# HGRN heads in seven pieces: transposes behind the level runs, the samples' work joined to the halves' turn-backs

## The chip, the cores and the metric

The kernel runs on one core of a Trainium2 chip. The metric is the device time of one execution in microseconds (us); less is better. The engines are named as the profile names them: PE (matrix products; PEld is its weight load), DVE (elementwise work), ACT (activations and copies), POOL (elementwise work), SP (issues most transfers). A change within about 0.2% (2.3 us) can't be told from no change here.

## The reference

One layer of a hybrid model on 1024 prompt tokens and 8 samples of 8 tokens: `h = x + W_out(concat[mLSTM(n), HGRN2(n)])` with `n = RMSNorm(x)`, then a last RMSNorm. Four mLSTM heads and eight HGRN2 heads, all in float32. Each HGRN2 head of 128 channels computes, in chunks:

```python
def step(S, inp):
    qc, kc, vc, fc = inp
    b = jnp.cumsum(fc, 2)
    diff = b[:, :, :, None, :] - b[:, :, None, :, :]
    D = jnp.exp(jnp.where(causal, diff, -jnp.inf))
    A = jnp.einsum('bhtk,bhsk,bhtsk->bhts', qc, kc, D)
    o = jnp.einsum('bhts,bhsv->bhtv', A, vc) + jnp.einsum('bhtk,bhkv->bhtv', qc * jnp.exp(b), S)
    kd = kc * jnp.exp(b[:, :, -1:] - b)
    S_new = jnp.exp(b[:, :, -1])[..., None] * S + jnp.einsum('bhsk,bhsv->bhkv', kd, vc)
    return S_new, o
```

Its output is normalised per head and multiplied into a gate `z`; the result goes through `W_out`. The outputs also hold the new states of prompt and samples.

## The kernel before

**Products.** A float32 product is made of three passes over split operands (`mm3`, L94 to L96: high by high, high by low, low by high), each at most 512 columns wide. The input projection takes most of PE's time.

**Two streams on PE.** For every head there is a *main* generator (`hgrn_main`, `mlstm_main`) that makes the head's own work in pieces and yields a weight after each, and a *side* generator that makes the projection of heads to come in steps of six products, and in the last head the beginning of the output stage. `weave` runs a piece of main, then as many side steps as its weight is worth. The heads run H0 M0 H1 M1 H2 M2 H3 M3 H4 H5 H6 H7 (H for HGRN2, M for mLSTM). The constant HEAD says what all weights of a head add up to. PE runs in the order in which the code is written. DVE, ACT, POOL and SP run in an order that a scheduler lays out by its own costs, each engine strictly in its order.

**An HGRN head's pieces.** First a burst of 32-wide products for level 1 of a tree of scores, then a run for levels 2 to 16 (`level_run(lower)`), each after DVE has made the levels' factors (`products`, L1030 to L1035). The nine transposes of the values (L1105) give `Vt`; ACT copies them (L1107) and makes the samples' masked copies VH, VL. `level_run(upper)` makes levels 32 and 64; ACT copies their scores into `A` (L1079). The keys, decayed on DVE into `KD` (L1110 to L1112), are turned by nine transposes (L1136) and copied by ACT into `KDt` (L1138) and, for the samples, into `KS` (L1142, subtracted on DVE at L1144). Then the prompt's state products (L1182) and the chain of eight states on DVE (L1190, L1192), whose last state SP stores (L1194). Then `outputs(0)` and `outputs(1)`, the two halves of the prompt (L1201, L1204), each normalised by `normed`: square on ACT (L1150), sum on DVE (L1152), root on POOL (L199, L200), multiply on DVE (L1154). The multiplied tile is turned back on PE (L1163, `turned`) and multiplied into `z` on DVE (L1211, `onto_z`). The samples' outputs are L1220 and L1225, their states L1232, L1233 (PE) and L1236 (DVE).

**Buffers.** PSUM pools: `lv` with two buffers (bursts, first transposes, turn-backs), `o` with three (states, outputs, values' transposes), `mm` with three (projection). A new tile waits for the last reader of the tile that held its buffer.

**What follows an HGRN head.** An mLSTM head begins with three loads on SP (RB L684, q L685, k L686); DVE adds into DT from RB (L691, L693); ACT takes Exp of DT and of RB (L694, L695), with a table load before the first and another before the sigmoid of `om` (L648) behind them. Later `pair_prep` loads `vr` (L704).

Of the kernel before, what the change touches and what calls it, by code (L numbers as in the profile page):

```python
# [13 lines left out]
ALU = mybir.AluOpType  # L14

P = 128
DM = 1024
T = 1088
# [12 lines left out]
def hybrid_step(  # L31
# [909 lines left out]
    def hgrn_main(h):  # L941
# [43 lines left out]
        def small_out(ps, o, li, n):  # L985
            W = MASKW[li]
            if li == 0:
                V.copy_predicated(A32, MK[0], ps[:, o:o + W])
            else:
                dst = A32[:, :2 * W].rearrange("p (g two n) -> p g two n", two=2, n=n)[:, :, 1, :]  # L990
                V.copy_predicated(dst, MK[li].rearrange("p (g n) -> p g n", n=n),
                                  ps[:, o:o + W].rearrange("p (g n) -> p g n", n=n))
# [12 lines left out]
        def rhs2(r, j):  # L1005
            if r == 4:
# [9 lines left out]
        ps = ps_lv()  # L1016
        burst(small_mms(ps, 0, K1[:, 0:512], k[:, TP:T], rhs1, 32)
              + small_mms(ps, 288, K1[:, 512:1024], k[:, TP:T], rhs2, 16), (q1, k1, k2))
        small_out(ps, 0, 0, 1)
        small_out(ps, 288, 1, 1)  # L1020
        late = [deferred.pop(0) for _ in range(len(deferred))]
# [14 lines left out]
                            hv(f, W, n)[:, :, 0, n - 1:n].to_broadcast([P, ng, n]), op=ALU.mult)  # L1036
            return n, Qn, Kn, last

        def level_run(group):
            ps = ps_lv()  # L1040
            mms, outs, o = [], [], 0
            for n, Qn, Kn, last in group:
                if n <= 16:
                    def rhs(r, j, Qn=Qn):
                        if r == 4:
                            return Qn[:, 512 + 16 * j:512 + 16 * j + 16]
                        return pairs(Qn, r * P + 16 * j, 112 - 32 * j, 2, 1, 16)

                    mms += small_mms(ps, o, Kn, Kn[:, 512:576] if n <= 4 else None, rhs, 16)
                    outs.append((n, o))  # L1050
                    o += MASKW[LEVELS.index(n) + 1]
                else:

                    for r in range(4):
                        for j in range(4):
                            b = 32 * j // n
                            odd, g = b % 2, (P // n - 1 - b if b % 2 else b) // 2
                            c = r * P + 64 * odd + n * g
                            mms.append((ps[32 * j:32 * j + 32, o + r * n:o + (r + 1) * n],
                                        Kn[:, r * P + 32 * j:r * P + 32 * j + 32], Qn[:, c:c + n], True, True))  # L1060
                    outs.append((n, o))
                    o += 4 * n
            burst(mms, (last,))
            for n, o in outs:
                if n <= 16:
                    small_out(ps, o, LEVELS.index(n) + 1, n)
                    if n == 16:

                        for j in range(4):
                            a = A[32 * j:32 * j + 32, 32 * j:32 * j + 1]  # L1070
                            dst = bass.AP(a.tensor, a.offset, [a.ap[0], [256, 4], [224 - 64 * j, 2], [1, 32]])
                            S.copy(dst, A32[32 * j:32 * j + 32, 0:256].rearrange("p (r e c) -> p r e c", e=2, c=32))  # L1072
                        for g in range(2):
                            S.copy(A[64 * g:64 * g + 32, TP + 32 * g:TP + 32 * g + 32], A32[64 * g:64 * g + 32, 256:288])
                else:
                    for b in range(P // n):
                        odd, g = b % 2, (P // n - 1 - b if b % 2 else b) // 2
                        c = P * odd + n * (2 * g + 1)
                        S.copy(A[n * b:n * b + n, 0:TP].rearrange("p (r c) -> p r c", r=4)[:, :, c:c + n],  # L1079
                               ps[n * b:n * b + n, o:o + 4 * n].rearrange("p (r c) -> p r c", r=4))  # L1080
# [8 lines left out]
            yield 3.3  # L1089
        upper = [products(16)]  # L1090
        yield 2.0
        level_run(lower)
        if h == 4:
            norm_states()
        yield 2.0
        for n in (32, 64):
            upper.append(products(n))
            yield 3.0
        V.tensor_tensor(q[:, :T], q[:, :T], f[:, :T], op=ALU.mult)
        Vt = unit("V")  # L1100
        for kk in range(3):
            pt = ps_o()
            for u in range(4 if kk < 2 else 1):
                t = kk * 4 + u
                PE.transpose(pt[:, u * P:(u + 1) * P], iT[:, t * P:(t + 1) * P], ident)  # L1105
            w = 512 if kk < 2 else P
            S.copy(Vt[:, kk * 512:kk * 512 + w], pt[:, :w])  # L1107
        KD = iT
        kdp = KD[:, :TP].rearrange("p (r two c) -> p r two c", two=2, c=P)
        V.tensor_tensor(kdp[:, :, 0, :], kp[:, :, 0, :], sfp[:, :, 0, :], op=ALU.mult)  # L1110
        V.tensor_tensor(kdp[:, :, 1, :][:, :, ::-1], kp[:, :, 1, :], sfp[:, :, 1, :], op=ALU.mult)
        V.tensor_tensor(twice(KD[:, TP:U]), once(k[:, TP:T]), once(Sf[:, TP:T]), op=ALU.mult)  # L1112

        Vs, VH, VL = half("Vs", F32R), half("VH", F32R), half("VL", F32R)
        S.copy(Vs[:, :P], Vt[:, TP:U])
# [8 lines left out]
        S0 = unit("S0")  # L1124
        S0v = S0[:, :1024].rearrange("p (b c) -> p b c", c=P)
        nc.sync.dma_start(out=S0v, in_=st_S[0, :, h].rearrange("b k v -> k b v"))
        yield 3.3
        level_run(upper)
        yield 3.4
        KDt = unit("KDt")  # L1130
        KS = two_groups()
        for kk in range(3):
            pt = ps_lv() if kk < 2 else ps_o()
            for u in range(4 if kk < 2 else 1):
                t = kk * 4 + u
                PE.transpose(pt[:, u * P:(u + 1) * P], KD[:, t * P:(t + 1) * P], ident)  # L1136
            if kk < 2:
                S.copy(KDt[:, kk * 512:(kk + 1) * 512], pt)  # L1138
            else:
                for g in range(2):  # L1140
                    r, c = slice(64 * g, 64 * g + 64), slice(g * P, (g + 1) * P)
                    S.copy(KS[r, c], pt[r, :P])  # L1142
                    r = slice(64 * g + 32, 64 * g + 64)
                    V.tensor_tensor(KS[r, c], pt[r, :P], f32(KS[r, c]), op=ALU.subtract)  # L1144
        yield 2.0

        def normed(ps, w):

# [9 lines left out]

        def turned(sq, w):

            tp = ps_lv()
            for u in range(w):
                PE.transpose(tp[:, u * P:(u + 1) * P], sq[:, u * P:(u + 1) * P], ident)  # L1163
            return tp
# [27 lines left out]
                V.scalar_tensor_tensor(Sn, states[-1], f[:, j * P + 127:j * P + 128], pk, op0=ALU.mult, op1=ALU.add)  # L1192
            states.append(Sn)
        nc.sync.dma_start(out=o_pS[0, 0, h], in_=states[7])  # L1194
        yield 3.2

        def outputs(hb):
            pq = ps_o()
# [13 lines left out]
            last_split(hb * 512, 512)  # L1212

        sq0 = outputs(0)
        yield 2.6
        sq1 = outputs(1)
        yield 2.6
        pq = ps_o()
        for j in range(4):
            PE.matmul(pq[32 * j:32 * j + 32, :P], lhsT=A[:, TP + win(j):TP + win(j) + 32],  # L1220
# [1 line left out]
        for e in range(2):  # L1222
            for j in range(4):
                b = 2 * j + e
                PE.matmul(pq[32 * j:32 * j + 32, :P], lhsT=qm[:, b * 64 + win(j):b * 64 + win(j) + 32], rhs=S0v[:, b, :],  # L1225
                          start=False, stop=e == 1)
        sq8 = normed(pq, 1)
        onto_z(sq0, 0)
        yield 2.6
        for g in range(2):  # L1230
            pk = ps_o()
            PE.matmul(pk, lhsT=KS[:, g * P:(g + 1) * P], rhs=VH[:, :512], start=True, stop=False)  # L1232
# [4 lines left out]
                                       pk[:, a * P:(a + 1) * P], op0=ALU.mult, op1=ALU.add)  # L1237
        nc.sync.dma_start(out=o_sS[0, :, h].rearrange("b k v -> k b v"), in_=S0v)
        onto_z(sq1, 1)
        yield 2.4  # L1240
        tp = turned(sq8, 1)
        zz, ts = compact(z[:, TP:T]), spread(tp[:, :P])
        for a in range(2):
# [133 lines left out]
            yield from g  # L1377

    STEPS = 48
    HEAD = {"H": 48.6, "M": 48.2}  # L1380

    def weave(side, main, ratio):

# [162 lines left out]
```

## Time and profile before

| what | value |
|---|---|
| median of 3 runs | 1164.46 us (1164.11 to 1165.91) |
| profiled execution | 1163.69 us |
| its span | 1161.9 us |
| mean granted PE clock | .993 |
| PE busy, 0 to 240 us | 216.06 |
| PE busy, 240 to 404 us | 162.57 of 164.00 |
| PE busy, 404 to 900 us | 491.96 of 496.00 |
| PE busy, 900 to 1162 us | 252.29 of 262.00 |
| DVE, ACT, POOL busy | 744.4, 467.4, 259.5 |

The profiled execution's time is its span and 1.8 us around it. PE is nearly full while the heads run (240 to 900 us), and has some 10 us idle in the last part, where the output stage waits for loads and splits. In the quoted rows, a start time in us is followed by the duration, engine, line, operation, `out<-in` with the program's names, and, in brackets, the idle time before it with what ended it. A row "x4" is four instructions in one, and starts with the first.

### The profile page before, as it was taken

How to read it: one execution, taken by the hardware profiler on the slowest of the kernel's cores; microseconds unless marked ns; L12 is line 12 of the kernel's file. 1: busy time of each engine (PE TensorE's matmuls, PEld its weight loads, DVE VectorE, ACT ScalarE, POOL GpSimd, SP SyncE). 2: the span in 40 equal slices, each digit the busy share in tenths (PEclk: the TensorE clock that was granted, in tenths of full speed). 3: DMA queues.
4: the chain of work that ended last, by engine and by line, in shares of the span. 5: the costliest groups of instructions: out<-in, count | busy, mean ns of one | idle time of the engine just before them, and what ended most of it. 6: DMA issues, size and time to landing. Idle time of an engine off the chain costs nothing.

```text
span 1161.9 us, 22940 instructions
## 1 busy us (share of the span) xinstructions
PE 1122.9 (97%) x9251; PEld 1055.8 (91%) x9251; DVE 744.4 (64%) x1474; ACT 467.4 (40%) x1045; POOL 259.5 (22%) x403
## 2 busy tenths in 40 slices
PE   5889999999999999999999999999999999999997
PEld 5789999899999999999999999999999997878886
DVE  4665354394778567784779467878677686644443
ACT  5454454426432443244422453252424344343332
POOL 4352443101530044203520153111020200100000
PEclk9889999999999999999999999999999999999999
DMA  7234343213324242324124331322222255475662
GB/s 238 70 120 142 118 147 122 76 45 115 102 81 151 63 147 78 117 94 135 56 78 151 118 108 60 133 74 77 56 77 56 76 162 151 143 231 163 200 188 95
DMA packets 154296, 134.05 MB, mean 115 GB/s; under 512 B 11515, under 2 KB 130391, under 8 KB 154190
## 3 DMA queue, kind: packets, MB, share of 16 engines
q1 hardware_dynamic: 154190, 132.59, 36.6%
q8 instruction: 73, 1.20, 0.4%
q14 instruction: 33, 0.27, 0.1%
HBM read 93.99 MB, written 38.57 MB: 114 GB/s over the span
## 4 chain that ended last, share of the span: by engine, by line
PE 78%; DVE 8%; ACT 5%; DMA 5%; issue 2%; SPq 0%; POOL 0%; POOLq 0%; DVEq 0%; ACTq 0%
PE mm L94 22%; PE mm L95 21%; PE mm L96 21%; PE lv L101 2%; DMA woraw<-in_w_out 1%; DMA mraw<-mixd 1%; ACT A L1079 1%; DMA RB<-rd 1%; ACT A L1072 1%; PE o L1182 1%; PE o L94 1%; PE o L96 1%; PE o L95 1%; PE o L1201 1%; PE o L1204 1%
## 5 line engine op out<-in xcount | busy, mean ns | idle before, releaser
L94 PE MATMUL mm<-XH,whi 128*128 128x384 f32 (+1 forms) x1344 | 451.7, 336 | 2.2 <-DVE xml L470 2.0
L95 PE MATMUL mm<-XL,whi 128*128 128x384 f32 (+1 forms) x1344 | 440.2, 328 | 0.0
L96 PE MATMUL mm<-XH,wlo 128*128 128x384 f32 (+1 forms) x1344 | 439.7, 327 | 0.0
L94 PEld LDWEIGHTS mm<-XH,whi 128*128 128x128 f32 x1344 | 253.8, 189 | 5.7 <-DVE xml L470 2.2
L95 PEld LDWEIGHTS mm<-XL,whi 128*128 128x128 f32 x1344 | 253.9, 189 | 1.6 <-issue 1.3
L96 PEld LDWEIGHTS mm<-XH,wlo 128*128 128x128 f32 x1344 | 253.3, 188 | 0.0
L147 POOL TENSOR_TENSOR wlo<-wraw,whi 128x1024 fp32r<-128x1024 f32 x34 | 83.0, 2442 | 108.6 <-ACT whi L147 108.4
L147 ACT CAST whi<-wraw 128x1024 fp32r<-128x1024 f32 x56 | 58.9, 1051 | 105.2 <-PE mm L95 84.7
L948 POOL MEMSET A<- 128x288 f32 x8 | 2.7, 342 | 251.0 <-ACT A L1072 251.0
L96 PE MATMUL mm<-XH,mlo 128*128 128x512 f32 x144 | 56.5, 392 | 1.1 <-DVE mlo L1295 1.0
L94 PE MATMUL mm<-XH,mhi 128*128 128x512 f32 x144 | 57.2, 397 | 0.2 <-ACT mhi L1294 0.2
L1294 ACT CAST mhi<-mraw 128x1024 fp32r<-128x1024 f32 (+1 forms) x32 | 31.8, 997 | 61.1 <-PE mm L95 38.6
L95 PE MATMUL mm<-XL,mhi 128*128 128x512 f32 x144 | 56.1, 390 | 0.0
L1295 DVE TENSOR_TENSOR mlo<-mraw,mhi 128x1024 fp32r<-128x1024 f32 (+1 forms) x32 | 36.9, 1155 | 24.7 <-ACT mhi L1294 24.5
L896 DVE TENSOR_SCALAR f<-f,OML,LB 128x384 f32<-128x384 f32 (+1 forms) x24 | 33.6, 1401 | 28.7 <-ACT f L894 28.6
L470 DVE TENSOR_TENSOR xml<-mm,xmh 128x384 fp32r<-128x384 f32 (+1 forms) x24 | 12.3, 511 | 51.0 <-ACT XB L469 48.0
L1363 POOL TENSOR_TENSOR rs<-rs,mhalf 128x1 f32<-128x1 f32 (+1 forms) x9 | 4.9, 542 | 147.7 <-DVE rs L1362 147.7
L96 PE MATMUL mm<-woh,mlo 128*128 128x512 f32 x96 | 37.5, 390 | 0.4 <-DVE mlo L1295 0.4
L95 PE MATMUL mm<-wol,mhi 128*128 128x512 f32 x96 | 37.4, 389 | 0.0
L94 PE MATMUL mm<-woh,mhi 128*128 128x512 f32 x96 | 37.3, 389 | 0.0
L199 POOL TENSOR_SCALAR oss<-oss 128x4 f32<-128x4 f32 (+1 forms) x24 | 4.6, 192 | 145.7 <-DVE oss L1152 145.7
L486 DVE SCALAR_TENSOR_TENSOR Y<-XB,PAR,Y 128x1112 f32<-128x1112 f32 x24 | 36.8, 1533 | 0.3
(349 smaller groups left out, 2217.1 us busy)
## 6 DMA issues: line engine op xcount, KB each, us to landing
wraw<-in_w_in SPq DMA_DIRECT2D x56, 512.0 KB
woraw<-in_w_out SPq DMA_DIRECT2D x16, 512.0 KB
mraw<-mixd SPq DMA_DIRECT2D x16, 512.0 KB
mraw<-mixd SPq DMA_DIRECT2D x16, 448.0 KB
xcd<-XB SPq DMA_DIRECT2D x8, 544.0 KB
qkd<-qk SPq DMA_DIRECT2D x16, 272.0 KB
xcr<-xcd SPq DMA_DIRECT2D x8, 544.0 KB
mixd<-xcr SPq DMA_DIRECT2D x8, 544.0 KB
```

The source lines that it names most:

```text
L94: PE.matmul(out, lhsT=lh, rhs=rh, start=first, stop=False)
L95: PE.matmul(out, lhsT=lh, rhs=rl, start=False, stop=False)
L96: PE.matmul(out, lhsT=ll, rhs=rh, start=False, stop=last)
L101: i = PE.matmul(out, lhsT=lhsT, rhs=rhs, start=start, stop=stop)
L147: return S.copy(hi, raw), eng.tensor_tensor(lo, raw, f32(hi), op=ALU.subtract)
L470: evs.append(V.tensor_tensor(ml[:, t0:t0 + m], ps[:, :m], f32(mh[:, t0:t0 + m]), op=ALU.subtract))
L486: V.scalar_tensor_tensor(Y[:, :1112], XB[:, j:j + 1112], cw[:, 8 * j + ft:8 * j + ft + 1], Y[:, :1112], op0=ALU.mult, op1=ALU.add)
L896: V.tensor_scalar(f[:, s], f[:, s], scalar1=OML[:, h:h + 1], scalar2=LB[:, h:h + 1], op0=ALU.mult, op1=ALU.add)
L1072: S.copy(dst, A32[32 * j:32 * j + 32, 0:256].rearrange("p (r e c) -> p r e c", e=2, c=32))
L1079: S.copy(A[n * b:n * b + n, 0:TP].rearrange("p (r c) -> p r c", r=4)[:, :, c:c + n], ps[n * b:n * b + n, o:o + 4 * n].rearrange("p (r c) - ...
L1294: S.copy(hi[:, :w * n], raw[:, :w * n])
L1295: V.tensor_tensor(lo[:, :w * n], raw[:, :w * n], f32(hi[:, :w * n]), op=ALU.subtract)
```

## The change

The pieces of an HGRN head go from eleven to seven:

1. the level-1 burst (for head 4 with `norm_states`, which was behind the lower run);
2. `level_run(lower)`, with the nine transposes of the values straight behind its burst;
3. `level_run(upper)`, with the nine transposes of the keys straight behind its burst; of their three PSUM tiles the first is in `lv` and two in `o` (before, two in `lv` and one in `o`);
4. the prompt's states;
5. `outputs(0)`;
6. `outputs(1)`, the samples' outputs, and the first half's turn-back;
7. the samples' states, the second half's turn-back, and that of the samples, whose tile is now in `o`.

The weights of the pieces change with it (their sum, HEAD, from 48.6 to 46.7), and the product of q and f on DVE goes behind the keys' products. No product is added or taken away.

```diff
@@ level_run @@
-        def level_run(group):
+        def level_run(group, then=None):
...
             burst(mms, (last,))
+            if then:
+                then()
@@ behind products(16) @@
-        level_run(lower)
-        if h == 4:
-            norm_states()
-        yield 2.0
+        Vt = unit("V")
+
+        def turn_values():
+            for kk in range(3):
+                pt = ps_o()
+                for u in range(4 if kk < 2 else 1):
+                    t = kk * 4 + u
+                    PE.transpose(pt[:, u * P:(u + 1) * P], iT[:, t * P:(t + 1) * P], ident)
+                w = 512 if kk < 2 else P
+                S.copy(Vt[:, kk * 512:kk * 512 + w], pt[:, :w])
+
+        level_run(lower, turn_values)
+        yield 2.6
         for n in (32, 64):
             upper.append(products(n))
             yield 3.0
-        V.tensor_tensor(q[:, :T], q[:, :T], f[:, :T], op=ALU.mult)
...
         V.tensor_tensor(twice(KD[:, TP:U]), once(k[:, TP:T]), once(Sf[:, TP:T]), op=ALU.mult)
+        V.tensor_tensor(q[:, :T], q[:, :T], f[:, :T], op=ALU.mult)
...
-        yield 3.3
-        level_run(upper)
-        yield 3.4
+        yield 3.8
...
-            pt = ps_lv() if kk < 2 else ps_o()
...
+        def turn_keys():
+            for kk in range(3):
+                pt = ps_o() if kk else ps_lv()
...
+        level_run(upper, turn_keys)
+        yield 3.2
...
-            tp = ps_lv()
+            tp = ps_lv() if w > 1 else ps_o()
...
         nc.sync.dma_start(out=o_pS[0, 0, h], in_=states[7])
-        yield 3.2
+        yield 4.2
...
         sq0 = outputs(0)
-        yield 2.6
+        yield 4.2
         sq1 = outputs(1)
-        yield 2.6
...
+        onto_z(sq0, 0)
         sq8 = normed(pq, 1)
-        onto_z(sq0, 0)
-        yield 2.6
+        yield 4.2
...
         onto_z(sq1, 1)
-        yield 2.4
         tp = turned(sq8, 1)
...
-    HEAD = {"H": 48.6, "M": 48.2}
+    HEAD = {"H": 46.7, "M": 48.2}
```

Line numbers shift: of those that the prediction names, L1079 is L1084 after, L1136 L1142, L1138 L1144, L1150 to L1154 are L1158 to L1162, L1163 is L1171, L1201 L1209, L1211 L1219, L1220 L1227, L1232 L1239; up to L960 nothing shifts.

The engines that a scheduler lays out are ordered anew. On ACT, where head 1 ends and the first exponentials of the second mLSTM head are taken (`osq` are the squares of the first half, the second half and the samples; DT and RB are the mLSTM head's; `om` is a sigmoid of the projection), before:

```order
L1150 ACTIVATE osq_4543<-o_4535 128x512
L648 ACTIVATE om_4509<-mm_4516 128x384
L1150 ACTIVATE osq_4573<-o_4564 128x512
L694 ACT_TABLE_LOAD
L694 ACTIVATE DT_4685<-DT_4685 128x1088
L695 ACTIVATE RB_4679<-RB_4679 128x1088
L1150 ACTIVATE osq_4605<-o_4592 128x128
L648 ACT_TABLE_LOAD
L648 ACTIVATE om_4509<-mm_4557 128x384
```

and after:

```order
L648 ACTIVATE om_4509<-mm_4516 128x384
L1158 ACTIVATE osq_4550<-o_4542 128x512
L694 ACT_TABLE_LOAD
L694 ACTIVATE DT_4685<-DT_4685 128x1088
L695 ACTIVATE RB_4679<-RB_4679 128x1088
L648 ACT_TABLE_LOAD
L648 ACTIVATE om_4509<-mm_4557 128x384
L1158 ACTIVATE osq_4592<-o_4583 128x512
L1158 ACTIVATE osq_4618<-o_4599 128x128
```

The second half's square stood ahead of the first table load, and now stands behind the two exponentials, the second table load and a sigmoid.

On DVE at the same place (`oss` are the sums of the squares), before:

```order
L1152 TENSOR_REDUCE oss_4545<-osq_4543 128x4
L1154 TENSOR_TENSOR osq_4543<-o_4535,oss_4545 128x512
L691 SCALAR_TENSOR_TENSOR DT_4685<-RB_4679,COLS,CF 128x128 x8
L693 SCALAR_TENSOR_TENSOR DT_4685<-RB_4679,COLS,CF 128x64
L1152 TENSOR_REDUCE oss_4575<-osq_4573 128x4
L1211 SCALAR_TENSOR_TENSOR z_3559<-lv_4612,PAR,z_3559 128x512
L800 TENSOR_REDUCE w_736_5288<-DT_4685 128x1
L1154 TENSOR_TENSOR osq_4573<-o_4564,oss_4575 128x512
```

and after:

```order
L1150 TENSOR_TENSOR KS_4387<-o_4451,KS_4387 32x128
L1200 SCALAR_TENSOR_TENSOR St_4499<-St_4499,f_3555,o_4489 128x128
L1200 SCALAR_TENSOR_TENSOR St_4499<-St_4499,f_3555,o_4494 128x128 x4
L1160 TENSOR_REDUCE oss_4552<-osq_4550 128x4
L691 SCALAR_TENSOR_TENSOR DT_4685<-RB_4679,COLS,CF 128x128 x8
L693 SCALAR_TENSOR_TENSOR DT_4685<-RB_4679,COLS,CF 128x64
L1162 TENSOR_TENSOR osq_4550<-o_4542,oss_4552 128x512
L800 TENSOR_REDUCE w_736_5288<-DT_4685 128x1
L1160 TENSOR_REDUCE oss_4594<-osq_4592 128x4
L1160 TENSOR_REDUCE oss_4620<-osq_4618 128x1
L1219 SCALAR_TENSOR_TENSOR z_3559<-lv_4612,PAR,z_3559 128x512
L1162 TENSOR_TENSOR osq_4592<-o_4583,oss_4594 128x512
```

The first half's multiply (L1154, now L1162) stood ahead of the nine DT sums, and now stands behind them; a subtraction for KS now stands inside the chain of the states.

On SP, where head 0 ends and the first mLSTM head's loads are issued, before:

```order
L140 DMA wraw_3359<-in_w_in 128x8x128
L1194 DMA out<-St_2958 128x128
L684 DMA RB_3139<-rd 128x1088
L685 DMA q_3137<-qkd 128x1088
L686 DMA k_3138<-qkd 128x1088
L614 DMA out<-co_3009 3x1024
L615 DMA out<-co_3009 24x1024
L704 DMA vr_3192<-vd 128x516
```

and after:

```order
L140 DMA wraw_3359<-in_w_in 128x8x128
L1202 DMA out<-St_2931 128x128
L704 DMA vr_3192<-vd 128x516
L684 DMA RB_3139<-rd 128x1088
L685 DMA q_3137<-qkd 128x1088
L686 DMA k_3138<-qkd 128x1088
L614 DMA out<-co_3089 3x1024
L615 DMA out<-co_3089 24x1024
```

The load of `vr` has moved from behind the three loads and two stores to ahead of them.

More of the change, by code (lines that the diff above doesn't have):

```diff
@@ L1018, in hgrn_main @@
               + small_mms(ps, 288, K1[:, 512:1024], k[:, TP:T], rhs2, 16), (q1, k1, k2))
+        if h == 4:
+            norm_states()
         small_out(ps, 0, 0, 1)
@@ L1098, in hgrn_main @@
             yield 3.0
-        V.tensor_tensor(q[:, :T], q[:, :T], f[:, :T], op=ALU.mult)
[L1100 to L1107, printed above, removed]
         KD = iT
@@ L1126, in hgrn_main @@
         nc.sync.dma_start(out=S0v, in_=st_S[0, :, h].rearrange("b k v -> k b v"))
-        yield 3.3
-        level_run(upper)
-        yield 3.4
+        yield 3.8
         KDt = unit("KDt")
         KS = two_groups()
-        for kk in range(3):
-            pt = ps_lv() if kk < 2 else ps_o()
[L1134 to L1145, printed above, removed]
+        def turn_keys():
+            for kk in range(3):
+                pt = ps_o() if kk else ps_lv()
+                for u in range(4 if kk < 2 else 1):
+                    t = kk * 4 + u
+                    PE.transpose(pt[:, u * P:(u + 1) * P], KD[:, t * P:(t + 1) * P], ident)
+                if kk < 2:
+                    S.copy(KDt[:, kk * 512:(kk + 1) * 512], pt)
+                else:
+                    for g in range(2):
+                        r, c = slice(64 * g, 64 * g + 64), slice(g * P, (g + 1) * P)
+                        S.copy(KS[r, c], pt[r, :P])
+                        r = slice(64 * g + 32, 64 * g + 64)
+                        V.tensor_tensor(KS[r, c], pt[r, :P], f32(KS[r, c]), op=ALU.subtract)
+        level_run(upper, turn_keys)
+        yield 3.2
         def normed(ps, w):
```

## The prediction

> **What bounds the kernel now.** I read the busy shares first, then the chain that ended last, then TensorE's waits.
>
> ```profile
> PE 1122.9 (97%) x9251; PEld 1055.8 (91%) x9251; DVE 744.4 (64%) x1474; ACT 467.4 (40%) x1045; POOL 259.5 (22%) x403
> PE 78%; DVE 8%; ACT 5%; DMA 5%; issue 2%; SPq 0%; POOL 0%; POOLq 0%; DVEq 0%; ACTq 0%
> PE lv L1136 <- ACT A L1079: 4.7, 8, 1.1
> PE o L1232 <- DVE osq L1154: 1.8, 3, 1.1
> PE mm L96 <- DVE mlo L1295: 1.4, 3, 0.7
> ```
>
> TensorE (PE) is busy 97% and holds 78% of the chain. The last three rows (line waited for, us in total, times, longest) are the waits in the code that the change touches. So the time is PE's instruction stream plus its waits, and a change that leaves every product in place can move only two things: the waits, and the seams where PE passes from one kind of product to another. I price both against the profiled execution, 1163.69 us, which is 0.77 us under the median of 1164.46.
>
> **Gain 1: the keys' transposes.** Around them, in head 1 (start, us, engine, line):
>
> ```profile
> 395.91 0.60 PE L1136 MATMUL lv<-CF,iT 128*128 128x128 f32 x4
> 397.00 0.66 PE L1136 MATMUL lv<-CF,iT 128*128 128x128 f32 x4 [0.48 <-ACT A L1079]
> 397.52 0.39 PE L94 MATMUL mm<-XH,whi 128*128 128x320 f32 x1
> 397.75 0.31 PE L95 MATMUL mm<-XL,whi 128*128 128x320 f32 x1
> 397.89 0.31 PE L96 MATMUL mm<-XH,wlo 128*128 128x320 f32 x1
> ```
>
> The second group of four waits for ACT to copy the upper levels' scores out (L1079), since that frees the second `lv` buffer. The change puts this group into the `o` pool, where nothing has been held since the values' transposes. From 397.00 to 397.52 five transposes take .52, so four take .42, and the start distance of 1.09 holds .67 of wait: .48 in the row and .19 inside the modelled end. Over 8 heads that is the 4.7 of the waits plus 8 x .19: **-6.2** (bounds -4.7 and -6.2).
>
> **Gain 2: seams.** Leaving the transposes, L94 to L95 takes .23 where .14 is the pace of the next pair. Entering a burst of 32-wide products costs the same:
>
> ```profile
> 391.59 0.34 PE L96 MATMUL mm<-XH,wlo 128*128 128x384 f32 x1
> 391.86 1.22 PE L101 MATMUL lv<-QK 128*32 128x32 f32 x96
> ```
>
> That is .27 against a pace of .17. Four pieces fewer per head are four such exits less, and the samples' 32-wide outputs, which now follow the second half's products directly, save an entry: five seams of .1 in 8 heads, **-4.0** (bounds 0, if the cost only moves to the joints inside a piece, and -4.0).
>
> **Loss 1: the end of heads 1 to 3, where an mLSTM head begins.** This term decides the sign. PE before, from the first half's outputs (S = 404.28) to the samples' states:
>
> ```profile
> 404.28 0.61 PE L1201 MATMUL o<-V,A 128*128 128x128 f32 x4
> 405.76 0.42 PE L94 MATMUL mm<-XH,whi 128*128 128x384 f32 x1
> 407.95 0.38 PE L1201 MATMUL o<-V,A 128*128 128x128 f32 x2
> 409.65 0.42 PE L94 MATMUL mm<-XH,whi 128*128 128x384 f32 x1
> 411.92 0.43 PE L1220 MATMUL o<-V,A 128*32 128x128 f32 x8
> 412.71 0.66 PE L1163 MATMUL lv<-CF,osq 128*128 128x128 f32 x4
> 413.12 0.43 PE L94 MATMUL mm<-XH,whi 128*128 128x384 f32 x1
> 415.12 0.39 PE L1232 MATMUL o<-VH,KS 128*128 128x512 f32 x1
> 415.59 0.42 PE L1232 MATMUL o<-VH,KS 128*128 128x512 f32 x1
> ```
>
> Before, 12 projection matmuls stand between each of these groups; after, 24 stand between the first half and the second, then second half, samples' outputs and the turn-back of the first half follow at once, then 24 of 320 columns, then the states. From the rows: 1.48 (outputs, 404.28 to 405.76), 24 matmuls at 2.19 per 12 less one seam = 4.28, second half 1.70, samples .79. The turn-back comes at S+8.2. It needs `sq0` multiplied on DVE (L1154, now L1162):
>
> ```profile
> 406.67 0.69 DVE L1152 TENSOR_REDUCE oss<-osq 128x4 f32<-128x512 f32 x1 [3.17 <-ACT osq L1150]
> 408.78 0.69 DVE L1154 TENSOR_TENSOR osq<-o,oss 128x512 f32<-128x512 f32 x1 [1.42 <-POOL oss L200]
> 409.71 2.19 DVE L691 SCALAR_TENSOR_TENSOR DT<-RB,COLS,CF 128x128 f32<-128x128 f32 x8 [0.24 <-DMA RB<-rd]
> 411.82 0.28 DVE L693 SCALAR_TENSOR_TENSOR DT<-RB,COLS,CF 128x64 f32<-128x64 f32 x1
> 530.27 6.33 DMA RB<-rd
> 657.17 6.94 DMA RB<-rd
> 530.51 0.61 PE L1201 MATMUL o<-V,A 128*128 128x128 f32 x4
> 657.41 0.61 PE L1201 MATMUL o<-V,A 128*128 128x128 f32 x4
> ```
>
> In the new DVE order the mLSTM head's DT sums (L691, L693) stand ahead of that multiply, and they wait for the load of RB. It landed at 409.7, 536.6 and 664.1, that is S+5.4, S+6.1 and S+6.7. I keep these distances: S moves 1.0 later by six more projection matmuls, but RB's load is queued behind the store of the last state, whose chain waits for the second KS subtraction in the new order and moves with it. DT takes 409.71 to 412.10 = 2.39, so S+7.8; the multiply .69: S+8.5 against S+8.2. PE waits .3, 1.0 and 1.6: **+2.9**.
>
> The larger wait is on ACT:
>
> ```profile
> 410.00 0.60 ACT L1150 ACTIVATE osq<-o 128x512 f32<-128x512 f32 x1 [2.40 <-PE o L1204]
> 412.18 1.28 ACT L694 ACT_TABLE_LOAD   x1 [1.59 <-DVE DT L693]
> 413.48 1.11 ACT L694 ACTIVATE DT<-DT 128x1088 f32<-128x1088 f32 x1
> 415.50 0.25 ACT L1150 ACTIVATE osq<-o 128x128 f32<-128x128 f32 x1
> 415.77 1.28 ACT L648 ACT_TABLE_LOAD   x1
> 417.06 0.49 ACT L648 ACTIVATE om<-mm 128x384 f32<-128x384 f32 x1
> ```
>
> Before, the second half's square (`sq1`, 410.00) ran ahead of the Exp pair. After, ACT holds table load, Exp, Exp, table load, `om`, and only then `sq1`'s square. The samples' second product group (the second L1232) needs the `o` buffer that the second half's outputs hold until `sq1` is multiplied. Chain: DT's end S+7.8; to the end of the second table load 417.06-412.10 less the samples' square (415.50 to 415.77) = 4.7; `om` some .44; square .60; from reduce to multiply 408.78-406.67 = 2.11; multiply .69; hand-over .1: **S+16.5**. PE gets there at S+8.2+.3 (its wait) +.41 (turn-back) +24 x .147 +.47 = **S+13.0**. The wait is 3.5 each time; where RB is later both sides move. **+10.5**, and the L1232 waits that it replaces go (1.8 less the .3 at head 0): **-1.5**. What is queued behind the Exp pair on ACT (`om`, then both squares) frees nothing else that PE asks for sooner.
>
> **Loss 2: head 0 into the first mLSTM head.** SP's order now has the load of `vr` ahead of RB, q and k:
>
> ```profile
> 277.40 0.38 SPq L684 DMA_DIRECT2D RB<-rd  x1
> 287.75 0.35 SPq L704 DMA_DIRECT2D vr<-vd  x1
> 302.71 0.28 PE L94 MATMUL o<-vhl,skl 128*128 128x258 f32 x1
> ```
>
> `vr` waits for a half buffer that a turn-back frees, at 287.75, ten us after RB was issued. RB would land at some 288.1+6.3 = 294.4, DT end at 296.8, the Exp pair at 300.3 (1.28 for the table and 1.11 for each Exp), and the scores' product and split follow before the `skl` product of 302.71: about level. Bounds 0 and 3; the chain leaves hardly anything, so **+2**.
>
> **Small terms.** The second KDt copy now queues on ACT behind the same score copies (L1079) for which PE waited before, so the states' products can wait in their place: bounds 0 and 4.7. Eighteen projection matmuls (2.6 us at .147) lie in between where nothing lay before, so I take a value near the lower end, **+.8**. The last head meets the output stage, whose splits PE already waits for (1.4 in the L1295 row): shifted pieces, **+1** (-1 to +3). Three edits I price at nothing, each by its cover. The values' transposes go straight behind the lower burst in the `o` pool, where no tile is live; PE has no row that waits for the copies of V, and its first reader, the states' products, comes 84 projection matmuls later. The product of q moves behind the keys' products on DVE; its first reader on PE is the first half's outputs, 42 projection matmuls (over 6 us at .147) later. The turn-back of the samples' outputs takes an `o` buffer in place of an `lv` one: it is the buffer of the samples' outputs themselves, whose last reader is the multiply that the turn-back waits for anyway.
>
> Sum: -6.2 -4.0 +2.9 +10.5 -1.5 +2 +.8 +1 = **+5.5**, so 1169.2 as the changed kernel's own profiled execution, and 1170.0 if the 0.77 is added for the median; between these two I take 1169.6.
>
> By the Trainium skill, "ScalarE: Activation LUTs", section "What ACT_TABLE_LOAD costs", a switch costs about 1.28 us and a drain of about 1.38 besides. Rows 412.18 and 413.48 contradict it here: the Exp starts 1.30 after the load began, so the load alone is priced; with drains the chain would be an estimated 2.8 us longer at each of three places.
>
> **Rivals.**
> *Covered boundary, faster.* The waits vanish if RB lands 3.5 us earlier, at S+1.9: S+16.5 becomes S+13.0. Then -10.2-1.5+3.8 = -7.9: **1156**. The three transfers took 5.7 to 6.9, so it needs a transfer of about 2 us or an earlier issue. 10%.
> *RB two us earlier, no change.* The turn-back waits go, and the three long ones become 1.5, 2.2 and 2.8: -10.2+6.5-1.5+3.8 = -1.4, **1162.3**; with one us, about 1166. The load could gain if PE and the stores near it are quieter. 18%.
> *Clock.* The waits of 3.5 us are long enough to lower PE's granted clock:
>
> ```profile
> 57.40:60.70 3.30, 0.28 (x2) 0.20 (x2) 3.30 (x3) 0.00 (x0) 3.30 (x2) 1.00 0.38 111
> 60.80:67.60 6.80, 5.42 (x23) 5.17 (x24) 4.56 (x10) 4.19 (x8) 1.39 (x2) 0.50 0.29 87
> ```
>
> After 3.3 us with PE nearly idle (.28 busy) the granted clock was .50 for 6.8 us. A PE-bound stretch would lose up to 3.4 us to it, at up to three places: +1.7 to +10.2, **1173 to 1179**. It decides when the wait reaches about 3.3 us with nothing in it, and mine is 3.5. 17%.
> The Trainium skill ("TensorE: Matmul & The Clock Gate", "HAM oscillation — how this bites in real kernels") says that PE's idle gaps should stay under some 3.4 us or the clock halves; the rows above agree, and by it these three waits stand right on the edge.
> *The order doesn't bite as listed:* only gain 2 and the small terms, 1160 to 1163; this would need ACT to be done with the Exp pair before `sq1`, and is in the 10% above.
>
> **How the numbers follow.** Forecast case (1166.8 to 1173) 55%, clock 17%, no change 18%, faster 10%. The range takes in the unknowns (head 0 by 0 to 3, end by -1 to 3, RB by one to two us) and half of the clock case: 1163 to 1177. About 0.2% (2.3 us) is what a measurement tells from no change: faster .11, same .17, slower .72.
>
> **What would show it.** Right: the L1136 wait on A gone; at heads 1 to 3 a row of some 3 x 3.5 us, the samples' states (L1239) waiting for `osq` L1162, and a short wait of L1171 on the same; ACT's Exp pair ahead of the second 128x512 square. Wrong: these waits under 1 us, RB landing near S+3, a wait of L1171 or of `o<-vhl,skl` far over 3 us, or a granted clock of .5 behind the waits.

## The result, and the profile after

| | median us | lowest to highest | runs |
|---|---|---|---|
| before | 1164.28 | 1163.49 to 1165.91 | 4 |
| changed | 1180.39 | 1177.82 to 1183.05 | 4 |

The ratio is 1.0133, 95% interval 1.0112 to 1.0154: slower by 16 us, where 5.3 were forecast, and above the range. The profiled execution took 1178.4 us, its span is 1176.6: 14.7 more than the span before.

The page of the changed kernel, busy shares and chain, and PE's waits (line waited for, us in total, times, longest):

```profile
PE 1124.7 (96%) x9251; PEld 1060.5 (90%) x9251; DVE 746.7 (63%) x1474; ACT 466.8 (40%) x1045; POOL 260.6 (22%) x403
PE 85%; DVE 5%; DMA 4%; ACT 4%; issue 2%; POOL 1%; SPq 0%; POOLq 0%; ACTq 0%; DVEq 0%
...
PE o L1239 <- DVE osq L1162: 10.9, 3, 3.6
PE lv L1171 <- DVE osq L1162: 4.4, 3, 2.1
...
PE o L94 <- DVE xr L1352: 2.2, 1, 2.2
...
PE o L96 <- DVE skl L727: 1.0, 1, 1.0
PE o L94 <- ACT skl L726: 0.9, 1, 0.9
...
PE mm L96 <- DVE mlo L1301: 0.3, 1, 0.3
```

PE's busy time is the same to 2 us. The keys' wait on A is gone, and two rows that are new or six times as long hold 15.3 us. The row of `xr` is new too; it belongs to the output stage, and the traces of all kernels with the changed last pieces have it (1.7 to 2.2 us). Head 1's end on PE, then on ACT, DVE and SP (start, us, engine, line):

```profile
405.61 0.61 PE L1209 MATMUL o<-V,A 128*128 128x128 f32 x4
411.36 0.38 PE L1209 MATMUL o<-V,A 128*128 128x128 f32 x2
416.16 0.63 PE L1171 MATMUL lv<-CF,osq 128*128 128x128 f32 x4 [2.06 <-DVE osq L1162]
420.14 0.39 PE L1239 MATMUL o<-VH,KS 128*128 128x512 f32 x1
424.42 0.47 PE L1239 MATMUL o<-VH,KS 128*128 128x512 f32 x1 [3.65 <-DVE osq L1162]
425.55 0.67 PE L94 MATMUL mm<-XH,whi 128*128 128x384 f32 x1
426.01 0.52 PE L95 MATMUL mm<-XL,whi 128*128 128x384 f32 x1
426.34 0.52 PE L96 MATMUL mm<-XH,wlo 128*128 128x384 f32 x1
```

```profile
415.49 1.28 ACT L694 ACT_TABLE_LOAD   x1 [7.52 <-DVE DT L693]
416.78 1.11 ACT L694 ACTIVATE DT<-DT 128x1088 f32<-128x1088 f32 x1
417.80 1.09 ACT L695 ACTIVATE RB<-RB 128x1088 f32<-128x1088 f32 x1
418.91 1.28 ACT L648 ACT_TABLE_LOAD   x1
420.21 0.49 ACT L648 ACTIVATE om<-mm 128x384 f32<-128x384 f32 x1
```

```profile
413.02 2.19 DVE L691 SCALAR_TENSOR_TENSOR DT<-RB,COLS,CF 128x128 f32<-128x128 f32 x8 [4.34 <-DMA RB<-rd]
415.13 0.28 DVE L693 SCALAR_TENSOR_TENSOR DT<-RB,COLS,CF 128x64 f32<-128x64 f32 x1
415.33 0.68 DVE L1162 TENSOR_TENSOR osq<-o,oss 128x512 f32<-128x512 f32 x1
```

```profile
404.62 0.37 SPq L140 DMA_DIRECT2D wraw<-in_w_in  x1
405.08 0.53 SPq L1202 DMA_DIRECT2D out<-St  x1
405.70 0.38 SPq L684 DMA_DIRECT2D RB<-rd  x1
```

Read from the bottom: SP issues RB's load behind a weight load and the store of the last state; it lands 7.3 us later; DVE, idle for 4.34 us, then makes DT and only then scales the first half (415.33); PE stands for the turn-back (416.16). ACT takes the exponentials behind DT, and PE stands again for the second half's buffer (424.42). That is the chain of the prediction, link by link. What its sum did not have are the last PE rows: behind the wait the projection runs at .33 a product (426.01 to 426.34), not .17. The windows of PE's busy time, with the granted clock third from the end; first one of the kernel before, then four of the changed one:

```profile
404.00:900.00 496.00, 491.96 (x4653) 479.10 (x4651) 358.60 (x798) 191.39 (x452) 120.07 (x181) 1.00 0.30 96
...
424.40:428.60 4.20, 4.18 (x17) 4.06 (x18) 4.20 (x13) 0.41 (x1) 2.71 (x2) 0.61 0.00 0
555.00:561.80 6.80, 5.63 (x19) 5.36 (x20) 5.09 (x14) 0.41 (x1) 3.86 (x4) 0.50 0.20 56
686.40:690.00 3.60, 0.00 (x0) 0.02 (x1) 2.36 (x6) 1.82 (x4) 2.25 (x5) 1.00 0.00 0
690.00:694.00 4.00, 3.98 (x24) 3.86 (x25) 4.00 (x12) 0.41 (x1) 2.73 (x2) 1.00 0.01 4
```

Before, the clock is whole while the heads run. In the changed kernel, head 1's wait was followed by a stretch at half clock, head 2's by a longer one; head 3's, just as long and entirely idle, by none.

Both kernels issue the same 4032 projection products in the same order, so the start of one and the same product in two traces says how far one kernel is behind. The differences between such points, chosen inside each mLSTM head (the first four stages end at products 1200, 1800, 2400 and 3050, the first begins at 840), inside heads H5 and H6 (3400, 3690), at the last one, and at the span's end, give the time by stage, changed less before:

| to 840 | H0 M0 | H1 M1 | H2 M2 | H3 M3 | H4 | H5 | H6 | behind the last product |
|---|---|---|---|---|---|---|---|---|
| -0.76 | +1.63 | +6.95 | +5.89 | +4.43 | -0.07 | -0.83 | -0.88 | -1.65 |

H5 and H6, with no mLSTM head behind or ahead of them, gain .83 and .88 us; H4, into which `norm_states` falls, gains nothing (its states' products take .24 longer, and its first half's outputs wait .28 for the states). The loss lies at the four places where an mLSTM head follows.

### The profile page after: what moved, and what is told of

Its sections match the earlier page's. It is cut to its first block, busy times and chain, and to the rows that moved or that the text cites. A ratio compares the mean times of both kernels' runs of the same rounds, so it can differ in the third digit from the quotient of the medians.

```text
span 1176.6 us, 22947 instructions
## 1 busy us (share of the span) xinstructions
PE 1124.7 (96%) x9251; PEld 1060.5 (90%) x9251; DVE 746.7 (63%) x1474; ACT 466.8 (40%) x1045; POOL 260.6 (22%) x403
## 4 chain that ended last, share of the span: by engine, by line
PE 85%; DVE 5%; DMA 4%; ACT 4%; issue 2%; POOL 1%; SPq 0%; POOLq 0%; ACTq 0%; DVEq 0%
PE mm L94 24%; PE mm L95 23%; PE mm L96 23%; PE lv L101 2%; DMA RB<-rd 2%; PE o L1190 1%; PE o L95 1%; PE o L94 1%; PE o L96 1%; PE o L1209 1%; PE o L1104 1%; PE o L1212 1%; PE lv L738 1%; DMA gB<-in_g_norm 1%; DVE DT L691 1%
```

## The experiments

Each kernel was timed against the kernel before on the same chip; ratios have their 95% interval. The median of before was 1165.5 beside the first four, then 1164.4, 1165.0 and 1165.1, with runs from 1161.3 to 1170.7.

| run | median us | ratio to before |
|---|---|---|
| after_again | 1181.1 | 1.0130 (1.0107 to 1.0153) |
| fill | 1176.5 | 1.0098 (1.0077 to 1.0119) |
| tail_only | 1177.1 | 1.0098 (1.0075 to 1.0120) |
| exp_held | 1169.6 | 1.0037 (1.0024 to 1.0050) |
| dt_held | 1166.2 | 1.0009 (0.9992 to 1.0026) |
| ordered | 1165.8 | 1.0004 (0.9990 to 1.0017) |
| front_only | 1164.1 | 0.9991 (0.9974 to 1.0008) |
| early | 1164.3 | 0.9989 (0.9974 to 1.0005) |
| front_ordered | 1161.4 | 0.9974 (0.9959 to 0.9989) |
| keypool | 1161.1 | 0.9970 (0.9958 to 0.9982) |
| early_vr | 1159.5 | 0.9957 (0.9941 to 0.9973) |
| early_kp | 1157.5 | 0.9930 (0.9903 to 0.9957) |
| early_front_vr | 1156.9 | 0.9928 (0.9909 to 0.9946) |
| early_front | 1157.8 | 0.9922 (0.9900 to 0.9944) |

### Does the halved clock cost anything? (after_again, fill)

The changed kernel again as a yardstick:

> The changed kernel once more, as the yardstick for the runs beside it. Theory A (late chain and clock: the scaling of the two halves stands behind the mLSTM head's DT sums and exponentials, PE waits 15.3 us for it in the profiled run, and the long waits halve PE's clock for 3.4 or 6.8 us): 1177 to 1184, the waits of L1171 and L1239 at 4 to 5 and 10 to 11 us, and runs that differ by 3 to 5 us by how many halvings they meet. Theory B (the merged pieces cost by themselves, at their joints): the same time, but a spread as narrow as before's.

1181.1. Its waits are 10.9 and 3.8, and this time all three long waits were followed by half clock: the stage H3 M3 costs 6.0 here and 4.4 in the first profile, where the third wait was not followed by it.

Then with products that nobody reads, in the place of the idle time:

```diff
             pk = ps_o()
+            if g == 0 and h in (1, 2, 3):
+                for _ in range(12):
+                    PE.matmul(pk, lhsT=KS[:, 0:P], rhs=VH[:, :512], start=True, stop=True)
             PE.matmul(pk, lhsT=KS[:, g * P:(g + 1) * P], rhs=VH[:, :512], start=True, stop=False)
```

> In heads 1 to 3, twelve products that nobody reads stand ahead of the samples' states, some 12 x .22 = 2.7 us of PE work in the place of the same length of idle time. If the clock costs what the profile shows (theory A): the waits of L1239 fall from 3.6 to about 1.0 each, no granted clock of .5 behind 240 us, and 4 to 6 us less than the changed kernel beside it, 1174 to 1177. If the halved clock costs nothing that counts: as the changed kernel, within 1.5 us. If PE was not really waiting there (against A): 8 us more, 1188.

1176.5, 4.6 under the yardstick (its runs take 1174.3 to 1178.8, those of the yardstick 1178.7 to 1181.9). PE's waits in it:

```profile
PE lv L1171 <- DVE osq L1162: 4.4, 3, 1.9
...
PE o L1242 <- DVE osq L1162: 2.8, 3, 0.9
```

36 products more, and the kernel is faster: the long waits fell from 10.9 to 2.8, which the added products fill (2.7 us a head), no head has half clock behind it, and what is saved is the clock's price: 1.2, 1.9 and 3.2 us in the stages H1 to H3, each compared with after_again. It was the rival, at 17%, that came true on top of the forecast.

### Is it the order on DVE and ACT? (ordered, exp_held, dt_held)

The DT sums are held behind the first half's scaling on DVE, the exponentials behind the samples' square (the last one made) on ACT:

```diff
-            S.activation(sq[:, :w * P], ps[:, :w * P], AF.Square)
+            i = S.activation(sq[:, :w * P], ps[:, :w * P], AF.Square)
+            ctxs["square"] = getattr(i, "ins", i)
...
-            V.tensor_tensor(sq[:, :w * P].rearrange("p (u c) -> p u c", c=P),
+            i = V.tensor_tensor(sq[:, :w * P].rearrange("p (u c) -> p u c", c=P),
...
+            ctxs.setdefault("scaled", getattr(i, "ins", i))
...
+        with tc.issue_after(ctxs.pop("scaled")):
+            for j in range(8):
+                V.scalar_tensor_tensor(DT[:, j * P:(j + 1) * P], RB[:, j * P:(j + 1) * P], COLS[:, j, h:h + 1],
...
+        with tc.issue_after(ctxs["square"]):
+            S.activation(DT[:, :T], DT[:, :T], AF.Exp)
+            S.activation(RB[:, :T], RB[:, :T], AF.Exp)
```

> The changed kernel with two orders held: the DT sums behind the first half's scaling on DVE, and the two exponentials behind the samples' square on ACT. Theory A: the 15.3 us of waits at L1171 and L1239 go, the halved clock with them, 1180.4 - 15.3 - 4.5 to 6 = 1159 to 1161, under the kernel before. Theory B: less than half of the loss goes, 1172 or more. Rival C (the exponentials, now later, become what the mLSTM head's first products wait for): the waits move there, 1165 to 1172, with rows o<-vhl,skl of over 1 us each at heads 1 to 3.

1165.8: 15.3 us less than the yardstick, not 20. The waits of the turn-back and of the samples' states are gone and the clock stays whole, but the time ends at that of the kernel before. Its PE waits have new rows:

```profile
PE o L94 <- DVE C L764: 2.2, 3, 0.9
...
PE o L95 <- DVE CC L772: 1.7, 4, 0.4
```

So PE waits at the mLSTM heads' state chain (C and its split CC), where rival C had it wait at the products on skl. That it is the later exponentials which cost here, as rival C said, is not shown by this; the next runs speak against it. By stage H1 to H3 are +1.2, +.4 and +.1 where -.83 each was to be had.

With the exponentials alone held:

> The changed kernel with the exponentials alone held behind the samples' square; the DT sums still stand ahead of the first half's scaling. Theory A: the waits of L1239 and the halved clock go, those of L1171 (4.4 us) stay: the run with both held, 1165.8, + 4.4 = 1170, some 4 us over the kernel before beside it. If the DT sums' place alone made both waits: 1178 or more.

1169.6, as theory A had it: the turn-back's wait stays (5.1 in its row), that of the samples' states goes. The halved clock did not go altogether: in the profiled execution, the slowest of twelve with 1175.3, it comes twice (from 308.6 and from 680.6), behind waits of .9 and 1.0, and of 1.9. With the DT sums alone held, the scheduler itself puts the second half's square ahead of the exponentials:

> The changed kernel with the DT sums alone held behind the first half's scaling; the scheduler then puts the second half's square ahead of the exponentials by itself, and the samples' square behind them. If ordered lost at the mLSTM heads because the exponentials stood behind the samples' square: 1161 to 1163. If RB's late landing is what they lose by (theory D): 1165 to 1166, as ordered.

1166.2, as ordered. Its waits are not quite the same:

```profile
PE o L1173 <- DVE osq L1163: 1.5, 3, 0.8
...
PE o L94 <- DVE C L763: 1.4, 3, 0.7
```

The exponentials now stand ahead of the samples' square. PE waits .8 us less at C than in ordered, and 1.5 for the samples' turn-back instead. So holding them behind that square costs nothing on balance, and most of the waits at C and CC (3.0 of 3.9) stay: something else holds the mLSTM heads. Theory D gave about the right number, but the run early, below, shows that it is not RB.

### Which half of the change? (tail_only, keypool, front_only, front_ordered)

The last pieces of the change on the kernel before (`outputs` to the end as changed, the transposes as before, HEAD 47.8):

> The kernel before with the last pieces of the change alone (outputs, samples and turn-backs joined, their weights); transposes as before. Theory A: the whole loss and no gain at the keys, 1164.3 + 13.7 + 4.5 = 1180 to 1186, waits of 3.5 at the samples' states. Theory B (the joined transposes cost): 1164 to 1170.

1177.1, below the range given but plainly theory A: 10.5 at the samples' states and half clock behind all three waits. Its turn-back waits only .2, where that of the whole change waits 4.4, so the merged front adds to the loss too. Undisturbed heads gain .2 by it.

One line alone:

```diff
-            pt = ps_lv() if kk < 2 else ps_o()
+            pt = ps_o() if kk else ps_lv()
```

> The kernel before with one edit: the second PSUM tile of the keys' transposes in the o pool in place of lv. Theory A (the keys' wait is PE time, .67 a head): 5.4 us less than the kernel before beside it, perhaps 4.5 if some of it comes back at the samples' states of heads 1 to 3, where RB then lands later against PE; the L1136 wait on A goes. Rival: the wait moves to the states' products, which need the copies KDt that queue on ACT behind the same score copies: within 1 us.

1161.1, ratio .9970 (-3.5 us): less than 5.4, since 1.3 us come back where the expectation named:

```profile
PE o L1232 <- DVE osq L1154: 3.1, 4, 1.0
```

By stage H5 and H6 gain .73 and .79.

The first half of the change on the kernel before (HEAD 47.5):

> The kernel before with the first half of the change alone (values' transposes behind the lower run, keys' behind the upper, their weights), the pieces of the end as before. Theory A: the gain of the changed kernel's undisturbed heads (.83 a head) less that of the tail alone (.2): .63 x 8 = 5 us less than before, less 1 to 2 us that come back at the samples' states: -3 to -5. Theory B (the joined pieces cost by themselves): no gain or slower.

1164.1, ratio .9991: no gain on the median, which is theory B's number, and runs from 1159.1 to 1169.7. H5 and H6 gain .73 and .79, just as by the one line: the joined pieces neither cost nor gain there. In H4 they cost 1.6 us (+.89, against -.71 with the one line); the first half's outputs wait there for the subtraction into KS (the second row below). The profiled execution is the slowest of the twelve, and shows what they lose:

```profile
PE o L1240 <- DVE osq L1162: 5.1, 3, 1.8
...
PE o L1209 <- DVE KS L1150: 1.5, 1, 1.5
```

```profile
414.80:418.20 3.40, 1.91 (x12) 1.47 (x10) 2.14 (x6) 3.02 (x3) 1.21 (x2) 1.00 0.27 79
...
418.60:422.00 3.40, 3.40 (x13) 3.10 (x14) 3.23 (x12) 2.28 (x4) 1.48 (x3) 0.50 0.00 0
```

Waits of 1.8, 1.8 and 1.5 at the samples' states, the first in a window in which PE was busy for 1.91 of 3.40, and half clock behind two of them. The mean granted clock of the twelve runs falls from .993 in the two fastest to .989 in the slowest, so how much half clock a run meets differs from run to run. With the held order:

> The same with the DT sums and the exponentials held behind the halves' scaling. If the held order only takes waits away: 1.5 to 2 us less than front_only. If, as in the run with the held order on the changed kernel, mLSTM heads 1 to 3 lose by later exponentials what the held order saves: 1 to 4 us more than front_only, with rows of o products waiting for C and CC.

1161.4, 2.7 under front_only: waits of 2.4 instead of 5.1, and no half clock behind them. That is somewhat more than the 1.5 to 2 expected. The loss at C and CC that ordered showed (3.9 us) is not there (.3). So it comes with the merged tail, not with the held order alone.

### What do the waits follow? (early, early_kp, early_front)

The loads of the coming mLSTM head are written ahead of the state chain, so that SP does not hold them behind the weight load and the last state's store:

```diff
+    def m_loads(h):
+        q, k, RB = unit("q"), unit("k"), unit("RB")
+        nc.sync.dma_start(out=RB[:, :T], in_=rd[h:h + 1, :].to_broadcast([P, T]))
+        nc.sync.dma_start(out=q[:, :T], in_=qkd[h, 0])
+        nc.sync.dma_start(out=k[:, :T], in_=qkd[h, 1])
+        ctxs[("loads", h)] = (q, k, RB)
...
+        if 0 < h < 4:
+            m_loads(h)
         states = []
         St = unit("St")
```

> The changed kernel with the three loads of mLSTM heads 1 to 3 (RB, q, k) written ahead of the HGRN head's state chain, so that on SP they stand ahead of the weight load and the store of the last state; the DT sums and the exponentials still stand ahead of the halves' scaling. Theory D (what PE waits for at heads 1 to 3 is RB's landing, and the order only decides where the wait is paid): the waits of L1171 and L1239 go, the halved clock too, and mLSTM heads lose nothing either: 1180 - 15.3 - 4.5 = 1160, 3 to 5 us less than the kernel before beside it. Theory A alone (the order is what costs): at least 7 us of the waits stay, since table loads, exponentials and sums take as long as before, 1168 or more.

1164.3: the waits of L1171 and L1239 and the half clock behind them are gone (one halving is left, at 435 to 439 us inside mLSTM head 1) although the scheduler still has the DT sums and exponentials first, so theory A alone falls; and yet it is not 1160: theory D falls short as well, since C and CC are waited for as in ordered (4.2 us) although RB's load is issued at 390.0, 15 us ahead of head 1's outputs, and DVE no longer waits for it. On the kernels with the old tail:

> The kernel before with the keys' second tile in the o pool and the same early loads. Theory D: the gain of the pool alone (-3.3) and the waits at the samples' states (3.1 in that run's profile): 6 us less than before, 1158. If RB's landing did not set those waits: as the pool alone, 1161.

> The first half of the change alone with the early loads. Theory D: its waits at the samples' states (5.1) and the halved clock go: 7 us less than front_only, 1157. If the larger pieces are worth something over the pool alone, some 1 to 2 us less than early_kp; if not, the same.

1157.5 and 1157.8, as theory D said, some .7 to .8% under the kernel before. Both beat both kernels, and they don't differ: the merged front is worth nothing measurable over the one line of keypool. With the same loads the merged tail stays .7% behind the old one (.9989 against .9922). Why, the trace of early shows, at mLSTM head 1, on SP (the first row is RB's early load), ACT and PE:

```profile
390.00 1.02 SPq L681 DMA_DIRECT2D RB<-rd  x1
...
422.90 0.39 SPq L1253 DMA_DIRECT2D out<-S  x1
423.34 0.57 SPq L140 DMA_DIRECT2D wraw<-in_w_in  x1
424.01 1.32 SPq L1261 DMA_DIRECT2D mixd<-z  x1
425.42 9.86 SPq L710 DMA_DIRECT2D vr<-vd  x3
```

```profile
431.06 0.62 ACT L712 CAST vhl<-vr 128x516 fp32r<-128x516 f32 x1 [4.04 <-DMA vr<-vd]
431.59 0.61 ACT L732 CAST skl<-sk 128x512 fp32r<-128x512 f32 x1
```

```profile
434.01 0.38 PE L94 MATMUL o<-vhl,skl 128*128 128x258 f32 x1 [0.98 <-DVE C L768]
```

The second load of `vr` is issued behind two stores that wait for the joined last piece; ACT waits 4.04 us for it, the split of skl queues behind that on ACT and DVE, the first C behind the split, and PE behind C. ACT's waits for vr add up to 11.7 us in early and 11.4 in ordered, in three waits each, and to 4.7 in early_front. So the same wait very likely holds the mLSTM heads in ordered; its removal was tried on early alone, in the next two runs.

### Is it that load? (early_vr, early_front_vr)

```diff
-        nc.sync.dma_start(out=o_sS[0, :, h].rearrange("b k v -> k b v"), in_=S0v)
+        def store_S():
+            nc.sync.dma_start(out=o_sS[0, :, h].rearrange("b k v -> k b v"), in_=S0v)
+
+        if 0 < h < 4:
+            ctxs["stores"] = [store_S]
+        else:
+            store_S()
...
         tiles += pair_prep(1)
+        if h:
+            with tc.issue_after(ctxs["vr"]):
+                for store in ctxs.pop("stores"):
+                    store()
```

> The run early (changed kernel, loads of RB, q and k early), and in heads 1 to 3 the stores of the samples' states and of z stand on SP behind the second load of vr, not ahead of it. Theory E (what still costs 1.8 us at each of mLSTM heads 1 to 3 is that vr's second load lands some 1.6 us later, behind two stores that wait for the joined last piece): the waits of o products for C and CC fall from 4.2 us to under 1.5, and the time is 4 to 5 us under early, ratio to before some .994 to .996. If these waits come from DVE or ACT work instead: as early, ratio .999, the C rows unchanged.

1159.5, 4.7 under early (by the ratios 3.7), and of the waits for C and CC one of .4 is left. SP now reads:

```profile
423.65 0.38 SPq L140 DMA_DIRECT2D wraw<-in_w_in  x1
424.13 0.52 SPq L710 DMA_DIRECT2D vr<-vd  x1
424.96 0.39 SPq L1259 DMA_DIRECT2D out<-S  x1
425.94 0.32 SPq L1272 DMA_DIRECT2D mixd<-z  x1
```

> The same move of the stores on early_front, whose vr loads are early already and which waits for C and CC only .5 us. Theory E: no more than 1 us better than early_front, ratio .991 to .993; it is the control. If moving these stores helps for another reason: as much as in early_vr.

The control: ratio .9928 against .9922, no gain. Theory E holds. By stage H1 to H3 in early_vr are -.6, -1.3 and -1.9; only H0 with M0, whose loads were left where they were, still loses (+1.6). So the merged tail stays about .3% behind the old one even then (.9957 against .9928, with intervals that touch), most of it at H0 with M0 (2.4 us between these two traces), where nothing was tried.

## Why the prediction was wrong, by its own steps

The working is that of the prediction; what it measured is taken from start distances and stages.

| term | forecast | measured |
|---|---|---|
| keys' wait | -6.2 | the row is gone (4.7); -.67 by start distances in head 5, -5.4 for eight such |
| seams | -4.0 | -1.3 |
| turn-back waits, H1 to H3 | +2.9 | +4.4 |
| long waits at the samples' states | +10.5 | +10.9 in the rows, 11.4 by start distances |
| the waits they replace | -1.5 | -1.5 in the rows, -1.9 by start distances |
| H0 into M0 | +2 | some +2.5 (+1.6 with head 0's own gain) |
| second KDt copy | +.8 | +1.0 |
| end | +1 | -1.7, with head 7's gain of .8 in it |
| halved clock | 0 (rival, 17%) | +4.2 |

The end is the least certain of these rows: in after_again, the same kernel, it is -2.1. With head 7's gain counted once, the measured terms add up to 14.0. The .4 at CC in the last mLSTM head and the .5 by which H4 falls short besides make it 14.9; from product 840 on, the changed kernel falls behind by 15.5 (14.7 and .76), so .6 stays unplaced.

**Right: the mechanism and its place.** The forecast had waits of 3.5 us at L1239 three times, behind the Exp pair; they are 3.65, 3.65 and 3.65. Both ends of that wait came some 2 us later than forecast in head 1 (PE was there at S+15.0 for S+13.0, the buffer was free at S+18.8 for S+16.5), because RB was later; the prediction had said that then both sides move. The keys' wait went, and came back at the states' products as far as forecast: the ninth of them waits for the second KDt copy, and the sixteen take 1.94 for 1.70 at heads 1 to 4. M0 waits for skl (the rows of 1.0 and .9) and CC, as costed. The table load was again followed by the exponential at once (415.49 to 416.78 is 1.29), so the load alone was the right price.

**Wrong: no price for the clock in the likeliest case.** "It decides when the wait reaches about 3.3 us with nothing in it, and mine is 3.5": by that sentence the rival's condition was met by the forecast itself, and its price belonged into the sum, not beside it. This is the step that failed: the sum has the wait at its length and the work behind it at full speed. From the rows of the changed kernel: 12 projection products behind head 3's wait take 2.17 (at full clock), behind head 1's 3.63 and behind head 2's 3.89, and the samples' products and turn-backs ahead of them 1.01, 1.13 and 1.91. That makes 1.6 and 2.6, together 4.2, the largest miss of any term; the yardstick has a third such stretch, and fill got back 4.6. Without half clock, in fill, the time lies inside the range that was forecast (1176.5).

**Wrong: seams.** The step took five exits of .1 a head as saved. Head 5's pieces, from the last projection product ahead to the pace regained, are .06 shorter for the values' piece, .78 for the keys' (of which .67 is the wait), .01 for the second half with the samples' outputs and .02 longer for the last: .16 in seams, not .5. The bound 0 of that step, "if the cost only moves to the joints inside a piece", was nearer than the value taken. The keys' piece shows it, in head 1: the four transposes behind the burst take .49 (395.72 to 396.21), where the prediction's working has .42 for four.

```profile
394.57 1.22 PE L101 MATMUL lv<-QK 128*32 128x32 f32 x96
395.72 0.66 PE L1142 MATMUL lv<-CF,iT 128*128 128x128 f32 x4
396.21 0.71 PE L1142 MATMUL o<-CF,iT 128*128 128x128 f32 x5
```

**Too small: the turn-back's waits.** "I keep these distances" (RB at S+5.4): RB landed at 413.0, which is S+7.4. The load took 7.3 us there, as against 5.7 before, and was issued at S+.1 (405.70) in place of S-.2:

```profile
404.04 0.38 SPq L684 DMA_DIRECT2D RB<-rd  x1
```

That row is of the kernel before. Head 1 makes the miss, with a wait of 2.06 for .3; heads 2 and 3 wait .65 and 1.70 for 1.0 and 1.6. Why the load took longer is not shown.

**Missing: a price for the mLSTM heads.** The second load of `vr` behind the stores of the joined last piece has no term. In the changed kernel it hardly shows (CC, .4 at the last mLSTM head; the other .4 is M0's), since PE is late there anyway; it came out only when the waits were taken away. Without these waits (3.9 us), ordered would have come out at an estimated 1162, below the kernel before.

The rival "covered boundary, faster" asked for RB 3.5 us earlier. In early it is issued 15 us earlier, and the waits went as the rival said; 1156 did not come, because PE then waited for C and CC behind the vr loads (1164.3, and 1159.5 in early_vr, where these waits are gone) and because H0 with M0 still loses.

## What to carry to other kernels

When pieces of an engine's stream are joined, the work of other engines behind them moves in one lump, and a scheduler may then put the next stage's long operations ahead of it: look at which small operation releases a buffer, and at what stands before it in its engine's queue and in the queue of loads. Test first whether one edit holds all of the gain (here a PSUM pool's name in one line, -.3%, and three loads written earlier, another -.4%). A long wait on PE is to be priced with the half clock that may follow (here 1.6 and 2.6 us behind waits of 3.65), not as the wait alone.

## What the runs showed of the hardware that was not expected

Whether the clock halves is not settled by the length of one wait. It halved behind 3.65 us of idle time at heads 1 and 2 and not behind the same at head 3 (686.4 to 690.0, PE busy 0.00 of 3.60, granted clock 1.00 for the 4 us that follow); in after_again it halved behind all three, and in tail_only behind waits of 3.66, 3.34 and 3.48. So eight of nine such waits were followed by half clock.

Shorter waits sometimes were. In front_only it halved behind a window in which PE was busy for 1.91 of 3.40 us, with no wait over 1.8. The waits for skl in mLSTM head 0 (.9 and 1.0) leave PE busy for about 1.6 of 3.4 us in eight traces; in one of them, exp_held, half clock followed. And in the changed kernel PE was busy for 1.34 of 3.40 us from 412.8 on, and full clock followed.

By the Trainium skill, "TensorE: Matmul & The Clock Gate", section "HAM oscillation — how this bites in real kernels", idle gaps over some 3.4 us are the ones to avoid. The runs agree that these are dangerous, and show in front_only that shorter ones are no safeguard. What decides it was not tried.
